# A two-layer decoder step on one core: heads' gate rows through DRAM, normalisers on GpSimd, the norm factors' row in two parts

## The chip, the cores and the metric

The kernel runs on one core of a Trainium2 chip. The metric is the device time of one execution in microseconds. Before the change the median of three runs is 953.47 us (953.25 to 953.63).

## The reference

The reference is one inference step of a two-layer decoder of width 1024, for a prompt of 256 tokens and for 8 samples of 8 new tokens each, with shared weights. Layer 0 mixes tokens by a gMLP (spatial gating in chunks of 128), layer 1 by an mLSTM matrix memory with eight heads. Each is followed by a gated MLP with a causal convolution, each part begins with an RMSNorm, and a last norm stands at the end. The memory layer, where most of the change lies, computes for each head and chunk:

```python
b = jnp.cumsum(fc, axis=-1)
D = b[..., :, None] - b[..., None, :] + ic[..., None, :]
inter = b + m[..., None]
m_t = jnp.maximum(inter, jnp.max(D, axis=-1))
w_intra = jnp.exp(D - m_t[..., None])
w_inter = jnp.exp(inter - m_t)
sc = jnp.einsum('bhtd,bhsd->bhts', qc, kc) * w_intra
num = w_inter[..., None] * jnp.einsum('bhtd,bhde->bhte', qc, C) + jnp.einsum('bhts,bhse->bhte', sc, vc)
den = w_inter * jnp.einsum('bhtd,bhd->bht', qc, n) + jnp.sum(sc, axis=-1)
h = num / jnp.maximum(jnp.abs(den), jnp.exp(-m_t))[..., None]
...
g = jnp.exp(bL[..., None] - b + ic - m_new[..., None])
kg = kc * g[..., None]
C_new = decay[..., None, None] * C + jnp.einsum('bhsd,bhse->bhde', kg, vc)
n_new = decay[..., None] * n + jnp.sum(kg, axis=2)
```

C is the state of 128 x 256 of a head and n its normaliser; both are outputs, for the prompt and for each sample.

## The kernel before

All 320 tokens are columns, and the features lie on the partitions. Weights stream from DRAM in blocks of 128 x 1024 (512 KB), issued by SyncE in the order of use. `take()` loads four blocks ahead and splits one ahead into a high and a low part of the fp32r format: ScalarE casts (`wh`, L167) and VectorE subtracts (`wl`, L168). `rows` (L189) makes three fp32r matmuls of each piece of 128 rows, and a `block` of eight such pieces is 24 matmuls of 320 columns into one bank of the pool `psm` (three banks, rows named `pm`). All other products go to the five banks of `psa`. The order of TensorE's instructions is that of the program. On the other engines the tile scheduler sets the order; `behind(...)` holds an instruction behind named ones.

**Norms.** Each norm sums squares over the features with TensorE (`norm_cols`, L242, tile `pc`) and takes the power −1/2 on GpSimd (`rc`, L254). `norm_row` (L270) turns the three columns of factors into a row on all partitions: VectorE puts them on diagonals (`dg`, L276 and L277), TensorE multiplies with ones (`pb`) and ScalarE copies the result (`rb`). It is called four times, once in each layer.

**Memory layer** (`layer_b`, L690). `gates` computes a matrix of 8 heads x 392 gate values (`Xf`: the running maximum of 320 tokens, 64 factors of the samples, 8 decays) and a second one, `RS`, that TensorE turns into columns (`pt`, `cols`). Then each head h runs through these steps, in a loop that works on the end of head h − 1 beside the start of head h:

- `qk_epi`, `v_epi`, `o_epi` end the weight blocks: convolution, activation, splits (`qh`, `kh`, `vTb`, `th_o`).
- `scores` spreads the head's row of `X` to all partitions with a matmul on a selector (`pMb`), forms the products `psc`, the weights `w` (exponentials on ScalarE, mask on GpSimd at L876), and their product `Pf` with its split `Ph`, `Pl` and sample parts `Pr`, `Ps`.
- `k_nat` and `v_nat` turn keys and values (`pk`, `pv`, written at L51) and scale them: `kz` (L916 and L917), `kgh` and `kgl` (L921, L922), `vh` and `vl` (L901, L902).
- `inter` and `state_sample` read the samples' states (`num`, `pcs`); `state_out` decays them (ScalarE, L957) and adds `pcs` (VectorE, L958). `numer` and `state_prompt` (`pCp`) follow; two small matmuls with `mkr` give the samples' normaliser sums, copied to `nPS`.
- `stats` takes mean, variance and scale (`sl` on GpSimd, L988), `nb` and the normed rows `hn`; `finish` turns these (`phn`), gates them (`y_b`) and splits them (`yhb` L1028, `ylb` L1029).

Heads 4 to 6 carry early blocks of the output product; after head 7 the rest follows.

Of the kernel before, what the change touches and what calls it, by code (L numbers as in the profile page):

```python
# [16 lines left out]
P = 128  # L17
# [21 lines left out]
class Net:  # L39
# [230 lines left out]
    def norm_row(self):  # L270

        nc = self.nc
        dg = self.tp.tile([P, T], F32, tag="sq", name="dg", bufs=2)
        pb = self.psa.tile([P, 512], F32, tag="pa", name="pb")
        for t in range(2):
            nc.vector.tensor_scalar(dg[:, t * P:(t + 1) * P], self.ident, self.rc[:, t:t + 1], None, op0=MULT)  # L276
        nc.vector.tensor_scalar(dg[:, TP:], self.ident[:, 64:], self.rc[:, 2:3], None, op0=MULT)  # L277
# [43 lines left out]
    def layer_a(self):  # L321
        nc, tc, I, O = self.nc, self.tc, self.I, self.O
        with tc.tile_pool(name="ya", bufs=1) as yp, tc.tile_pool(name="la", bufs=1) as lp:
# [80 lines left out]
            for q in range(4):  # L404
                pv = [self.psa.tile([P, 512], F32, tag="pa", name="pv") for _ in range(2)] + \
                    [self.psm.tile([P, 512], F32, tag="pm", name="pvs")]
                k = 0
                while k < KD:
                    (wh, wl), kn = self.take()
                    wh, wl = [x.rearrange("p (k e) c -> p k (e c)", e=4) for x in (wh, wl)]  # L410
                    for i in range(kn):
                        if q == 0 and k + i + 1 < KD:
                            self.enter(k + i + 1)
                        columns(q, k + i, pv, wh[:, i, :], wl[:, i, :])
                    k += kn
# [12 lines left out]
                if q > 0:  # L428
                    v_gelu(q, pv)
                waiting = pv  # L430
# [259 lines left out]
    def layer_b(self):  # L690
# [5 lines left out]
        with ExitStack() as ctx:  # L696
# [7 lines left out]
            X = lp.tile([P, 392], F32R, name="X")  # L704
            sel = lp.tile([P, NH, P], F32R, name="sel")
# [5 lines left out]
            nPS = lp.tile([P, NH, 10], F32, name="nPS")  # L711
            mkr = lp.tile([P, NB], F32R, name="mkr")
# [12 lines left out]
            def gates(rp):  # L725
# [3 lines left out]
                selr = rp.tile([40, NH, P], F32, name="selr")  # L729
# [5 lines left out]
                nc.sync.dma_start(selr, I["sel"])  # L735
# [4 lines left out]
                nc.gpsimd.memset(X.bitcast(F32), 0.0)  # L740
                nc.gpsimd.memset(sel.bitcast(F32), 0.0)
# [8 lines left out]
                Xf = row("Xf", 392)  # L750
# [46 lines left out]
                nc.scalar.activation(RS[32:40, 0:T], g, AF.Exp)  # L797
                nc.scalar.activation(RS[64:72, 0:T], m, AF.Exp, scale=-1.0)
# [5 lines left out]
                ps = self.block(KD, self.x_rhs)  # L804
                pt = self.psa.tile([P, 512], F32, tag="pa", name="pt")
# [48 lines left out]
            def scores(h):  # L854
# [3 lines left out]
                pb = self.psa.tile([P, 512], F32, tag="pa", name="pMb")  # L858
                mm(pb[:, :392], sel[:, h, :], X, True, True)
# [4 lines left out]
                dec = decs[:, h, :]  # L864
                nc.scalar.copy(dec, pb[:, 384:392])
# [6 lines left out]
                for (o, c0, t) in ((0, 0, 0), (TP, P, 1)):  # L872
                    nc.scalar.activation(w[:, o:o + TP - c0], pb[:, c0:TP], AF.Exp, scale=-1.0, bias=colsT[:, t, h:h + 1])
                nc.scalar.activation(w[:, 384:], w[:, 384:], AF.Exp, scale=-1.0)
                for o in (0, TP):
                    nc.gpsimd.affine_select(w[:, o:o + P], w[:, o:o + P], pattern=[[1, P]], compare_op=ALU.is_ge, fill=0.0,  # L876
                                            base=0, channel_multiplier=-1)
                Pf = hp.tile([P, 448], F32, tag="Pf", name="Pf", bufs=1)
# [3 lines left out]
                nc.vector.scalar_tensor_tensor(Pf, sc[:, :448], 0.25 * KSC, w, op0=MULT, op1=MULT)  # L882
                self.split(Ph, Pl, Pf[:, :384])

# [4 lines left out]
                s["P"] = (Ph, Pl, dec)  # L889
# [14 lines left out]
            def k_nat(h, bank=None):  # L904
                s = S[h]
                ks = s["k"][0]
                pk = bank or self.psa.tile([P, 512], F32, tag="pa", name="pk")
                for t in range(3):
                    self.tr(pk[:, t * P:(t + 1) * P], ks[:, t * P:(t + 1) * P] if t < 2 else s["ks"], self.ident)
                kgh = hp.tile([P, 2, P], F32R, tag="kgh", name="kgh", bufs=1)  # L910
                kgl = hp.tile([P, 2, P], F32R, tag="kgl", name="kgl", bufs=1)
                kz = hp.tile([P, 2, P], F32R, tag="kz", name="kz", bufs=1)
                src = pk[:, 2 * P:3 * P]

                for i in range(2):
                    nc.scalar.activation(kz[:, i, :], src, AF.Copy, scale=gm[:, i, h:h + 1])  # L916
                    nc.vector.scalar_tensor_tensor(kz[:, i, :], src, gm[:, 2 + i, h:h + 1], kz[:, i, :].bitcast(F32), op0=MULT, op1=ADD)  # L917
                for t in range(2):
                    g = colsT[:, t, 32 + h:33 + h]
                    src = pk[:, t * P:(t + 1) * P]  # L920
                    nc.scalar.activation(kgh[:, t, :], src, AF.Copy, scale=g)  # L921
                    nc.vector.scalar_tensor_tensor(kgl[:, t, :], src, g, kgh[:, t, :].bitcast(F32), op0=MULT, op1=SUB)  # L922
                s["kg"] = (kgh, kgl, kz)

# [50 lines left out]
            def stats(h):  # L975
# [12 lines left out]
                nc.gpsimd.tensor_tensor(sl, rd, self.mhalf.to_broadcast([P, 3]), op=ALU.pow)  # L988
                nb = hp.tile([P, 3], F32, tag="nb", name="nb", bufs=1)
# [5 lines left out]
            def state_prompt(h):  # L995
# [19 lines left out]
            def finish(h):  # L1015
# [3 lines left out]
                for e in range(2):  # L1019
# [9 lines left out]
                    nc.vector.scalar_tensor_tensor(yl[:, e, :], y, g, yh[:, e, :].bitcast(F32), op0=MULT, op1=SUB)  # L1029
# [51 lines left out]
            k_nat(0)  # L1081
            v_nat(0)
            for h in range(1, NH):
# [10 lines left out]
                if h == 1:  # L1094
                    hand_over(0)
                qk_epi(h, 1, ps)
# [3 lines left out]
                if h == 1:  # L1100
                    close(0)
                else:
                    with self.behind_split():
                        stats(h - 1)
                v_epi(h, 0, ps)
                early(h, 2)
                if h == 1:
                    stats(0)
                else:
                    with self.behind(S[h]["halves"][1]):  # L1110
                        self.prefetch(0, self.used + 2)
                with self.behind(*S[h]["halves"]):
                    ps = blk()
                v_epi(h, 1, ps)
# [13 lines left out]
                v_nat(h)  # L1128
                if h == 1:
                    finish(0)  # L1130
                if not last:
                    with self.behind(S[h]["vh"], S[h]["vl"]):
                        ps = blk()
                    o_epi(h, 1, ps)
                    hand_over(h)
# [15 lines left out]
            nc.gpsimd.tensor_tensor(nS, nS, nPS[:, :, 2:], op=ADD)  # L1151
            nc.sync.dma_start(O["nP"], nPS[:, :, 0])
# [64 lines left out]
def _lay_out(i):  # L1217
# [64 lines left out]
    sel = np.zeros((40, NH, P), f)  # L1282
    for h in range(NH):
        sel[h, h] = 1.0
        sel[32 + h, h] = 1.0
    a["sel"] = sel
# [33 lines left out]
```

## Time and profile before

| | |
|---|---|
| median of three runs | 953.47 us |
| the profiled execution | 953.45 us |
| its span, first to last instruction | 951.7 us |
| TensorE clock granted | 0.998 |
| busy: TensorE, VectorE, ScalarE, GpSimd | 945.0, 670.9, 519.1, 83.9 us |
| one head of the memory layer (the third) | 27.85 us |

In the profile PE is TensorE's matmul, PEld its weight load, DVE VectorE, ACT ScalarE, POOL GpSimd and SP SyncE. A row of the timeline gives start and length in us, engine, line, operation, output and inputs by the program's names, partitions x elements, and a count of equal neighbours; in square brackets stand the idle time ahead of it and what ended it. Matmuls overlap, so their cost is read from start to start.

### The profile page before, as it was taken

The numbers are of one execution on the slowest core, as the hardware profiler recorded it, in microseconds if no ns is written. First come the engines' busy times: TensorE is split into PE (matmuls) and PEld (weight loads), VectorE is DVE, ScalarE is ACT, GpSimd is POOL, SyncE is SP. The second block draws the span as 40 slices with busy tenths as digits, with TensorE's granted clock in tenths as the row PEclk, the third lists the DMA queues.
The fourth block names the chain that finished last, engine by engine and source line by source line (L and its number), as shares of the span: only waits on it lengthen the run. The fifth ranks groups of instructions, "written<-read, shape, count | busy, mean of one in ns | idle before, by whom it ended". The sixth has DMA issues, their size and how long they took to land.

```text
span 951.7 us, 17271 instructions
## 1 busy us (share of the span) xinstructions
PE 945.0 (99%) x6571; PEld 923.4 (97%) x6571; DVE 670.9 (70%) x1237; ACT 519.1 (55%) x952; POOL 83.9 (9%) x277
## 2 busy tenths in 40 slices
PE   9999999999999999999999999999999999999997
PEld 8789999999999999999999999999999999999997
DVE  6568985577777764458898987776777777775542
ACT  6467444354455543347787776575755555444332
POOL 2200000010000000012211001000101111100001
PEclk9999999999999999999999999999999999999999
DMA  8646344444444445456557556634474444445621
GB/s 286 212 133 186 122 140 150 144 150 150 143 151 156 151 147 148 145 179 215 183 209 224 167 193 205 202 116 163 112 246 156 153 155 146 144 148 152 200 83 56
DMA packets 58073, 155.25 MB, mean 163 GB/s; under 512 B 7670, under 2 KB 19574, under 8 KB 57990
## 3 DMA queue, kind: packets, MB, share of 16 engines
q1 hardware_dynamic: 57846, 153.89, 50.6%
q8 instruction: 52, 0.85, 0.4%
q14 instruction: 31, 0.25, 0.1%
q10 hardware_dynamic: 144, 0.26, 0.1%
HBM read 142.19 MB, written 11.94 MB: 162 GB/s over the span
## 4 chain that ended last, share of the span: by engine, by line
PE 99%; POOLq 0%; ACT 0%; DVE 0%; DVEq 0%; issue 0%; ACTq 0%
PE pm L48 83%; PE pv L48 5%; PE num L48 2%; PE pvs L48 2%; PE pyt L48 1%; PE pmix L48 1%; PE py L48 1%; PE pCp L48 1%; PE psc L48 1%; PE pcs L48 1%; PE pv L51 1%; PE phn L51 0%; PE pw L48 0%; PE pk L51 0%; PE pc L48 0%; PE pg L48 0%
## 5 line engine op out<-in xcount | busy, mean ns | idle before, releaser
L167 ACT CAST wh<-raw 128x1024 fp32r<-128x1024 f32 (+4 forms) x252 | 254.3, 1013 | 286.7 <-PE pm L48 170.2
L48 PE MATMUL pm<-xh,wh 128*128 128x320 f32 x1216 | 379.5, 312 | 0.0
L168 DVE TENSOR_TENSOR wl<-raw,wh 128x1024 fp32r<-128x1024 f32 (+4 forms) x252 | 295.9, 1179 | 118.5 <-ACT wh L167 116.0
L48 PE MATMUL pm<-xh,wl 128*128 128x320 f32 x1216 | 375.8, 309 | 0.0
L48 PE MATMUL pm<-xl,wh 128*128 128x320 f32 x1216 | 375.6, 309 | 0.0
L48 PEld LDWEIGHTS pm<-xh,wh 128*128 128x128 f32 x1216 | 228.4, 188 | 0.7
L48 PEld LDWEIGHTS pm<-xl,wh 128*128 128x128 f32 x1216 | 228.4, 188 | 0.2
L48 PEld LDWEIGHTS pm<-xh,wl 128*128 128x128 f32 x1216 | 228.3, 188 | 0.0
L48 PE MATMUL pm<-yh_f,wh 128*128 128x320 f32 x308 | 95.3, 309 | 0.0
L48 PE MATMUL pm<-yl_f,wh 128*128 128x320 f32 x308 | 94.9, 308 | 0.0
L48 PE MATMUL pm<-yh_f,wl 128*128 128x320 f32 x308 | 94.9, 308 | 0.0
L48 PEld LDWEIGHTS pm<-yl_f,wh 128*128 128x128 f32 x308 | 57.8, 188 | 0.0
L48 PEld LDWEIGHTS pm<-yh_f,wh 128*128 128x128 f32 x308 | 57.8, 188 | 0.0
L48 PEld LDWEIGHTS pm<-yh_f,wl 128*128 128x128 f32 x308 | 57.8, 188 | 0.0
L536 DVE SCALAR_TENSOR_TENSOR fcv<-fpad,vecs,fcv 128x336 f32<-128x336 f32 x88 | 49.6, 565 | 2.2 <-ACT fcv L534 0.7
L301 DVE TENSOR_TENSOR xT<-pm,xT 128x320 f32<-128x320 f32 x38 | 18.6, 490 | 31.7 <-PE pm L48 31.7
L48 PE MATMUL pm<-yhb,wh 128*128 128x320 f32 x128 | 40.2, 314 | 0.0
L48 PE MATMUL pm<-yh_a,wh 128*128 128x320 f32 x128 | 39.6, 309 | 0.0
L48 PE MATMUL pm<-yh_a,wl 128*128 128x320 f32 x128 | 39.5, 309 | 0.0
L48 PE MATMUL pm<-yl_a,wh 128*128 128x320 f32 x128 | 39.5, 308 | 0.0
L48 PE MATMUL pm<-ylb,wh 128*128 128x320 f32 x128 | 39.5, 308 | 0.0
L48 PE MATMUL pm<-yhb,wl 128*128 128x320 f32 x128 | 39.4, 308 | 0.0
(317 smaller groups left out, 1356.8 us busy)
## 6 DMA issues: line engine op xcount, KB each, us to landing
raw<-in_f_up SPq DMA_DIRECT2D x88, 512.0 KB, 3.5
raw<-in_b_win SPq DMA_DIRECT2D x48, 512.0 KB, 4.7
raw<-in_f_dn SPq DMA_DIRECT2D x28, 448.0 KB, 3.2
C<-in_C SPq DMA_DIRECT2D x32, 258.0 KB, 5.4
raw<-in_a_win SPq DMA_DIRECT2D x16, 512.0 KB, 3.8
raw<-in_a_wo SPq DMA_DIRECT2D x16, 512.0 KB, 3.6
out_Cs<-C SPq DMA_DIRECT2D x32, 256.0 KB, 5.7
raw<-in_f_dn SPq DMA_DIRECT2D x14, 512.0 KB, 3.5
```

Source lines behind the costliest of these rows:

```text
L48: self.pin(self.nc.tensor.matmul(out, lhsT, rhs, start=start, stop=stop))
L51: self.pin(self.nc.tensor.transpose(out, in_, ident))
L167: self.last_split = nc.scalar.copy(wh[:, c, :], raw[:, c, :])
L168: self.last_low = nc.vector.tensor_tensor(wl[:, c, :], raw[:, c, :], wh[:, c, :].bitcast(F32), op=SUB)
L301: self.nc.vector.tensor_tensor(x, ps[:, :T], x, op=ADD)
L536: nc.vector.scalar_tensor_tensor(cv, pd[:, i:i + NC], self.vec(w + i * KF), cv, op0=MULT, op1=ADD)
```

## The change

1. **`norm_row`**: the factors are split in a high and a low fp32r part, with a diagonal for each, and two fp32r matmuls replace the one in full precision. In layer A the call moves behind the next group of columns.
2. **`gates`**: the first three matmuls of the first q block stand ahead of the column sums. `X`, `sel` and `mkr` go, with their loads, fills and casts. Head 0's row is spread by a full-precision matmul of `Xf`, on 128 partitions with zeros, with a selector `first`, ahead of the turns `pt`.
3. **Rows through DRAM**: `Xf` and a part of `RS` are written to a tensor `rows` of 8 x 456 in DRAM; `rows_in(h)` reads one head's row back onto all partitions (tile `mb`, two buffers), a head ahead. `scores(h)` reads it in place of `pMb` for h > 0.
4. **Normalisers**: the matmuls with `mkr` go. GpSimd multiplies the samples' keys with the row's factors (`nk`, 128 x 64), copies the decays (`decs`) and the prompt's normaliser (`nP`). At the end VectorE sums `nk` and adds.
5. **Order**: the later half of `scores` becomes `weigh`; `pk` takes a bank of `psm` in all heads; `v_nat(h)` follows `finish(h − 1)` from head 2 on; in the last head `finish(6)` stands ahead of `weigh(7)`; in head 1 `stats(0)` is cut in two and `hand_over` moves.

```diff
     def norm_row(self):
-        dg = self.tp.tile([P, T], F32, tag="sq", name="dg", bufs=2)
+        rc = self.tp.tile([P, 2, 3], F32R, tag="rc2h", name="rc_hl", bufs=1)
+        self.split(rc[:, 0, :], rc[:, 1, :], self.rc)
+        dg = self.tp.tile([P, 2, T], F32R, tag="dg", name="dg", bufs=1)
+        rc = rc.bitcast(F32)
+        for half in range(2):
+            nc.vector.tensor_tensor(
+                dg[:, half, :TP].rearrange("p (t c) -> p t c", c=P), self.ident.unsqueeze(1).to_broadcast([P, 2, P]),
+                rc[:, half, :2].unsqueeze(2).to_broadcast([P, 2, P]), op=MULT)
+            nc.vector.tensor_scalar(dg[:, half, TP:], self.ident[:, 64:], rc[:, half, 2:3], None, op0=MULT)
...
-        self.mm(pb[:, :T], self.ones, dg, True, True)
+        for half in range(2):
+            self.mm(pb[:, :T], self.ones.bitcast(F32R), dg[:, half, :], half == 0, half == 1)
...
                 if q == 1:
-                    self.norm_row()
                     load_ws()
                 if q == 2:
+                    self.norm_row()
                     row_sums()
...
+                p0 = self.psm.tile([P, 512], F32, tag="pm", name="pm")
+                (wh, wl), _ = self.take()
+                self.rows(p0, wh, wl, 1, self.x_rhs, True, False)
                 self.norm_cols()
-                p0 = self.block(KD, self.x_rhs)
+                self.rows(p0, wh[:, 1:, :], wl[:, 1:, :], 7, lambda k: self.x_rhs(1 + k), False, True)
                 self.norm_row()
...
-                nc.vector.tensor_copy(X[0:8], Xf)
-                nc.vector.tensor_tensor(X[32:40], Xf, X[0:8].bitcast(F32), op=SUB)
-                nc.scalar.copy(sel[:40], selr)
-                nc.vector.tensor_copy(mkr, mk[:, :NB])
+                nc.sync.dma_start(I["rows"][:, :392], Xf)
...
+                nc.sync.dma_start(I["rows"][:, 392:], RS[32:40, TP:T])
+                rows_in(0)
+                rows_in(1)
...
                 ps = self.block(KD, self.x_rhs)
+                pb = self.psa.tile([P, 512], F32, tag="pa", name="pMb")
+                mm(pb[:, :392], first, Xz, True, True)
+                S[0]["spread"] = pb
                 pt = self.psa.tile([P, 512], F32, tag="pa", name="pt")
...
-                pb = self.psa.tile([P, 512], F32, tag="pa", name="pMb")
-                mm(pb[:, :392], sel[:, h, :], X, True, True)
+                rows = s["rows"]
+                pb = s.get("spread", rows)
...
+                if h:
+                    with self.behind(s["masked"]):
+                        sums(h)
...
+            def sums(h):
+                s = S[h]
+                if h:
+                    nc.gpsimd.tensor_copy(decs[:, h, :], s["rows"][:, 384:392])
+                nc.gpsimd.tensor_tensor(nk[:, h, :], s["k"][0][:, TP:T], s["rows"][:, 392:], op=MULT)
+
+            def weigh(h):
+                Ph, Pl, _ = S[h]["P"]
+                Pf, Pr = S[h]["Pf"]
                 self.split(Ph, Pl, Pf[:, :384])
...
+            def rows_in(h):
+                S[h]["rows"] = lp.tile([P, 456], F32, tag="mb", name="mb", bufs=2)
+                nc.sync.dma_start(S[h]["rows"], I["rows"][h:h + 1, :].to_broadcast([P, 456]))
...
-                for i in range(2):
-                    mm(pc[:, CW:CW + NB], kz[:, i, :], mkr, i == 0, i == 1)
-                Cp = hp.tile([P, DV], F32, tag="Cp", name="Cp", bufs=1)
-                nc.scalar.copy(Cp, pc[:, :DV])
-                nc.sync.dma_start(O["Cp"][h], Cp)
-                nc.scalar.copy(nPS[:, h, :], pc[:, DV:DV + 10])
+                Cp = hp.tile([P, CW], F32, tag="Cp", name="Cp", bufs=1)
+                nc.scalar.copy(Cp, pc[:, :CW])
+                nc.sync.dma_start(O["Cp"][h], Cp[:, :DV])
+                nc.gpsimd.tensor_copy(nP[:, h:h + 1], Cp[:, DV:DV + 1])
...
             scores(0)
-            k_nat(0)
+            k_nat(0, self.psm.tile([P, 512], F32, tag="pm", name="pk"))
             v_nat(0)
+            with self.behind(S[0]["vl"]):
+                weigh(0)
...
+                if not last:
+                    rows_in(h + 1)
                 v_epi(h, 0, ps)
...
                 scores(h)
-                k_nat(h, self.psm.tile([P, 512], F32, tag="pm", name="pk") if h == 1 else None)
+                if last:
+                    finish(h - 1)
+                weigh(h)
+                k_nat(h, self.psm.tile([P, 512], F32, tag="pm", name="pk"))
+                if 1 < h and not last:
+                    finish(h - 1)
                 if h > 1:
-                    finish(h - 1)
+                    v_nat(h)
...
-            nc.gpsimd.tensor_tensor(nS, nS, nPS[:, :, 2:], op=ADD)
-            nc.sync.dma_start(O["nP"], nPS[:, :, 0])
+            ns = lp.tile([P, NH, NB], F32, name="ns")
+            with self.behind(S[h]["yl"]):
+                nc.vector.tensor_reduce(ns, nk.rearrange("p h (b s) -> p h b s", s=NS), axis=mybir.AxisListType.X, op=ADD)
+            nc.vector.scalar_tensor_tensor(nS, ns, 0.5 * KSC, nS, op0=MULT, op1=ADD)
+            nc.sync.dma_start(O["nP"], nP)
```

How this moves instructions is seen at three places. The first is TensorE in the gates, from the last matmuls of the gate block (`pg`) over the column sums (`pc`) into the first q block (`pm`). Before:

```order
L48 MATMUL pg<-xh,wl 128x320
L48 MATMUL pg<-xl,wl 128x320
L48 MATMUL pc<-ones,acc 128x2 x3
L48 MATMUL pm<-xh,wh 128x320
L48 MATMUL pm<-xl,wh 128x320
L48 MATMUL pm<-xh,wl 128x320
```

After, at the same place:

```order
L48 MATMUL pg<-xh,wl 128x320
L48 MATMUL pg<-xl,wl 128x320
L48 MATMUL pm<-xh,wh 128x320
L48 MATMUL pm<-xl,wh 128x320
L48 MATMUL pm<-xh,wl 128x320
L48 MATMUL pc<-ones,acc 128x2 x3
```

The three matmuls of the first piece of the q block have moved ahead of the column sums.

The second place is VectorE in head 0, from the second product with the convolution's taps to the last low part of the keys (`kgl`). Before:

```order
L831 SCALAR_TENSOR_TENSOR bcv<-bpad_4513,vecs,bcv 128x344
L882 SCALAR_TENSOR_TENSOR Pf<-psc,w 128x448
L917 SCALAR_TENSOR_TENSOR kz<-pk,gm,kz 128x128
L902 SCALAR_TENSOR_TENSOR vl<-pv,rc_4619,vh 128x256
L310 TENSOR_TENSOR Pl<-Pf,Ph 128x384
L886 SCALAR_TENSOR_TENSOR Ps<-Pf,mk,Pr 128x4x16
L922 SCALAR_TENSOR_TENSOR kgl<-pk,cols,kgh 128x128
L902 SCALAR_TENSOR_TENSOR vl<-pv,rc,vh 128x256
L922 SCALAR_TENSOR_TENSOR kgl<-pk,cols,kgh 128x128
```

After (line numbers are those of the changed file), from the weight split and the copy of `cols` on; between the two pieces the dots leave out `Qz`, `w`, `gm` and two `vl`:

```order
L168 TENSOR_TENSOR wl<-raw,wh 128x1024
L819 COPY cols<-pt 128x288
...
L899 SCALAR_TENSOR_TENSOR Pf<-psc,w 128x448
L944 SCALAR_TENSOR_TENSOR kz<-pk,gm,kz 128x128
L929 SCALAR_TENSOR_TENSOR vl<-pv,rc,vh 128x256
L316 TENSOR_TENSOR Pl<-Pf,Ph 128x384
L944 SCALAR_TENSOR_TENSOR kz<-pk,gm,kz 128x128
L914 SCALAR_TENSOR_TENSOR Ps<-Pf,mk,Pr 128x4x16
L842 SCALAR_TENSOR_TENSOR bcv<-bpad_4521,vecs,bcv 128x344
L834 TENSOR_TENSOR bpad_4517<-pm,rb 128x256
L949 SCALAR_TENSOR_TENSOR kgl<-pk,cols,kgh 128x128
```

The last `vl` and both `kz` now stand ahead of the first `kgl`; in before one `vl` stood between the two `kgl`, and one split fewer stood ahead of the copy of `cols`.

The third place is ScalarE in head 2, around the casts of values (`vh`) and keys (`kgh`). Before:

```order
L921 ACTIVATE kgh<-pk,cols 128x128 x2
L901 ACTIVATE vh<-pv,rc 128x256
L901 ACTIVATE vh<-pv,rc_4619 128x256
L1012 ACTIVATE th_o<-o_b 128x320
L901 ACTIVATE vh<-pv,rc 128x256
L167 CAST wh<-raw 128x1024 x3
```

After:

```order
L928 ACTIVATE vh<-pv,rc_4632 128x256
L928 ACTIVATE vh<-pv,rc 128x256
L948 ACTIVATE kgh<-pk,cols 128x128
L887 ACTIVATE w<-mb,cols 128x256
L1064 ACTIVATE yhb<-y_b,gnh 128x320
L948 ACTIVATE kgh<-pk,cols 128x128
L887 ACTIVATE w<-mb,cols 128x128
L928 ACTIVATE vh<-pv,rc 128x256
L167 CAST wh<-raw 128x1024
```

The exponentials of head 3 (`w`, from the row `mb` that DRAM gave) stand here between the casts of head 2; in before a head's exponentials stood ahead of its own `kgh`.

More of the change, by code (lines that the diff above doesn't have):

```diff
@@ L710, in layer_b @@
             decs = lp.tile([P, NH, NB], F32, name="decs")
-            nPS = lp.tile([P, NH, 10], F32, name="nPS")
-            mkr = lp.tile([P, NB], F32R, name="mkr")
+            nP = lp.tile([P, NH], F32, name="nP")
+            nk = lp.tile([P, NH, 64], F32, name="nk")
             pads = []
@@ L728, in gates @@
                 rst = rp.tile([40, 2, T], F32, name="rst")
-                selr = rp.tile([40, NH, P], F32, name="selr")
+                Xz = rp.tile([P, 392], F32, name="Xf")
+                first = rp.tile([P, P], F32, name="first")
                 RS = rp.tile([P, T], F32, name="RS")
@@ L749, in gates @@
                 ig, z, az = zi[:8], zi[32:], az[32:]
-                Xf = row("Xf", 392)
+                Xf = Xz[:8]
+                nc.gpsimd.memset(Xz, 0.0)
+                nc.gpsimd.memset(first, 0.0)
+                nc.gpsimd.memset(first[0:1, :], 1.0)
                 a, M = RS[0:8, 0:T], Xf[:, 0:T]
@@ L863, in scores @@
                 mm(sc[:, 384:448], s["ks"], q[:, TP:T], True, True)
-                dec = decs[:, h, :]
-                nc.scalar.copy(dec, pb[:, 384:392])
+                dec = rows[:, 384:392]
+                if h == 0:
+                    dec = decs[:, 0, :]
+                    nc.scalar.copy(dec, pb[:, 384:392])
                 Qd = Qz.rearrange("p (g i r) -> p g i r", g=4, i=2)[:, :, :, :NS]
@@ L988, in stats, with scaled @@
                 nc.gpsimd.tensor_tensor(sl, rd, self.mhalf.to_broadcast([P, 3]), op=ALU.pow)
+                s["sl"] = num, mv, sl
+                if h:
+                    scaled(h)
+            def scaled(h):
+                s = S[h]
+                num, mv, sl = s.pop("sl")
                 nb = hp.tile([P, 3], F32, tag="nb", name="nb", bufs=1)
@@ L1095, in layer_b @@
                     hand_over(0)
+                    with self.behind(S[0]["masked"]):
+                        sums(0)
                 qk_epi(h, 1, ps)
@@ L1108, in layer_b @@
                     stats(0)
-                else:
-                    with self.behind(S[h]["halves"][1]):
-                        self.prefetch(0, self.used + 2)
+                with self.behind(S[h]["halves"][1]):
+                    self.prefetch(0, self.used + 2)
                 with self.behind(*S[h]["halves"]):
                     ps = blk()
+                if h == 1:
+                    with self.behind_split():
+                        scaled(0)
                 v_epi(h, 1, ps)
                 scores(h)
-                k_nat(h, self.psm.tile([P, 512], F32, tag="pm", name="pk") if h == 1 else None)
+                if last:
[4 more added lines that the diff above has]
+                    finish(h - 1)
                 if h > 1:
-                    finish(h - 1)
+                    v_nat(h)
                 early(h, 3)
@@ L1281, in _lay_out @@
     a["seg"] = seg
[L1282 to L1286, printed above, removed]
     tok = s // 32 * 16 + s % 16
@@ L1304 @@
     O = {k: nc.dram_tensor("out_" + k, s, F32, kind="ExternalOutput").ap() for k, s in _OUTS.items()}
+    I["rows"] = nc.dram_tensor("rows", (8, 456), F32, kind="Internal").ap()
     with tile.TileContext(nc) as tc:
```

29 lines of the change are left out of this document (13 added, 16 removed).

## Prediction

> **What bounds the kernel now.** I read the page first: the busy time of each engine and the chain that ended last.
>
> ```profile
> span 951.7 us, 17271 instructions
> PE 945.0 (99%) x6571; PEld 923.4 (97%) x6571; DVE 670.9 (70%) x1237; ACT 519.1 (55%) x952; POOL 83.9 (9%) x277
> ...
> PE 99%; POOLq 0%; ACT 0%; DVE 0%; DVEq 0%; issue 0%; ACTq 0%
> ...
> L168 DVE TENSOR_TENSOR wl<-raw,wh 128x1024 fp32r<-128x1024 f32 (+4 forms) x252 | 295.9, 1179 | 118.5 <-ACT wh L167 116.0
> ```
>
> TensorE works 945.0 of 951.7 us and carries 99% of the chain. A mean over stages can hide one with another limit, so I then asked for the waits of TensorE and for the windows of one head of the memory layer.
>
> ```profile
> PE pw L48 <- PEq L1302: 0.8, 1, 0.8
> ```
>
> ```profile
> 486.80:514.65 27.85, 27.85 (x221) 26.93 (x220) 25.53 (x58) 21.94 (x52) 4.38 (x11) 1.00 0.65 212
> ```
>
> The columns of the second are the stretch, its length, then busy time of PE, PEld, DVE, ACT, POOL, then granted clock, DMA share and GB/s. In this head TensorE is busy for all 27.85 us, VectorE for 25.53 and ScalarE for 21.94. So the memory layer is TensorE's too, but VectorE has only 2.3 us to spare in a head. The list of waits shows one, at the start; but ends of matmuls are modelled, so a short wait hides in a "busy" row. I therefore take prices and hidden waits from **start to start** of neighbouring rows. The rule for the sum: a matmul removed is time removed, unless a new wait takes it; work on the other engines is free as long as what it makes is ready when TensorE gets there.
>
> **Change, part by part.**
>
> *The factors' row.* TensorE's rows around one of the four calls:
>
> ```profile
> 197.26 0.31 PE L48 MATMUL pm<-xh,wl 128*128 128x320 f32 x1
> 197.41 0.70 PE L48 MATMUL pb<-dg,ones 128*128 128x320 f32 x2
> 197.71 0.56 PE L48 MATMUL pm<-xh,wh 128*128 128x320 f32 x1
> 198.10 0.30 PE L48 MATMUL pm<-xl,wh 128*128 128x320 f32 x1
> ```
>
> One fp32r matmul of 320 columns steps 197.41 − 197.26 = 0.15 us. The full-precision product is recorded as two matmuls; from its start to the second block matmul behind it is 198.10 − 197.41 = 0.69, less one ordinary step, 0.54. Two fp32r matmuls are 2 × 0.15 = 0.29 (0.147 unrounded). Each call saves 0.25, four save **−1.0**. The price is the diagonal, made twice and after a cast and a subtraction. The tightest call is that of the gates:
>
> ```profile
> 427.78 0.85 POOL L254 TENSOR_TENSOR rc<-ms,mhalf 128x3 f32<-128x3 f32 x1 [0.17 <-DVE ms L253]
> ...
> 428.66 0.48 DVE L276 TENSOR_SCALAR dg<-ident,rc 128x128 f32<-128x128 f32 x2 [0.88 <-POOL rc L254]
> 429.06 0.25 DVE L277 TENSOR_SCALAR dg<-ident,rc 128x64 f32<-128x64 f32 x1
> ```
>
> ```profile
> 430.26 0.70 PE L48 MATMUL pb<-dg,ones 128*128 128x320 f32 x2
> ```
>
> The diagonal is ready at 429.31 and used at 430.26: 0.95 us of cover. A half costs VectorE the same 0.65 (428.66 to 429.31); a cast and a subtraction of three columns in a row, some 0.3 to 0.4. In the gates the whole starts about 0.2 later (below) and TensorE arrives about 0.25 earlier, so the first half comes about on time and the second (needed 0.15 later) 0.1 to 0.2 late. The bounds are no wait and, if each call lost the whole 0.25 again, +1.0. I take +0.1 here and +0.1 in layer A, where a weight split now stands behind the moved call, +0.2 together.
>
> *The normaliser's matmuls.* Each of eight heads loses two:
>
> ```profile
> 486.66 0.28 PE L48 MATMUL pCp<-mkr,kz 128*128 128x8 f32 x2
> 486.80 0.40 PE L48 MATMUL pm<-xh,wh 128*128 128x320 f32 x1
> 487.03 0.31 PE L48 MATMUL pm<-xl,wh 128*128 128x320 f32 x1
> ```
>
> From their start to the second matmul behind them is 0.37, less one step of 0.15: 0.22 a head, **−1.8** for eight. Their work goes to GpSimd, whose cost is a rival below.
>
> *The heads' rows.* Heads 1 to 7 lose the matmul that spreads a head's row:
>
> ```profile
> 497.45 0.34 PE L48 MATMUL pMb<-X,sel 128*128 128x392 f32 x1
> 497.63 0.28 PE L48 MATMUL psc<-qh,kh 128*128 128x256 f32 x1
> ```
>
> 0.18 each, seven of them: **−1.26**. The scores then start 0.18 earlier and need their k split so much sooner. Head 0 spreads its row in full precision. No such matmul of 392 columns is in the trace: below it lies the 0.18 above (no loss), above it four times that, 0.72; the nearest row is the full-precision pb, 0.54 × 392/320 = 0.67 by width. I take 0.67, so **+0.49**.
>
> *The gates' first matmuls* now stand ahead of the column sums:
>
> ```profile
> 425.56 0.41 PE L48 MATMUL pg<-xl,wl 128*128 128x320 f32 x1
> 425.97 0.83 PE L48 MATMUL pc<-ones,acc 128*128 128x2 f32 x6
> ```
>
> The sums start 0.41 after the last matmul of the gates instead of 0.15: TensorE waits 0.26 for the squares. Three block matmuls (0.44) fill it and put the sums 0.18 later: **−0.26**, between that and nothing.
>
> *Head 0's states* wait in before; head 1 shows the same work without most of the wait:
>
> ```profile
> 458.00 1.08 PE L48 MATMUL num<-C,Qz 128*32 128x258 f32 x16
> 459.00 0.90 PE L48 MATMUL pcs<-vh,kz 32*128 32x256 f32 x4
> ...
> 460.19 0.41 PE L48 MATMUL pm<-xh,wh 128*128 128x320 f32 x1
> ```
>
> ```profile
> 479.31 1.08 PE L48 MATMUL num<-C,Qz 128*32 128x258 f32 x16
> ...
> 481.00 0.42 PE L48 MATMUL pm<-xh,wh 128*128 128x320 f32 x1
> ```
>
> 2.19 against 1.69, so 0.50 of wait. What comes late is on VectorE:
>
> ```profile
> 458.60 0.48 DVE L902 SCALAR_TENSOR_TENSOR vl<-pv,rc,vh 128x256 fp32r<-128x256 f32 x1
> 459.12 0.35 DVE L922 SCALAR_TENSOR_TENSOR kgl<-pk,cols,kgh 128x128 fp32r<-128x128 f32 x1
> ```
>
> The last kgl ends at 459.47 and frees the bank of pk, which pcs takes. After the change pk lies in another pool, and on VectorE the last vl and kz stand ahead of both kgl. Against it, one more weight split (1.18, L168 of the page) stands ahead of the copy of cols. Adding up the rows in the new order brings the last kz to about 458.4; TensorE wants it at about 459.0. I take the gain, **−0.50**; the bounds are that, and a further 0.6 lost if the split is not absorbed.
>
> *The last head.* TensorE's rows around the late half of an output operand:
>
> ```profile
> 671.43 0.31 PE L48 MATMUL pm<-yhb,wh 128*128 128x320 f32 x1
> 671.65 0.41 PE L48 MATMUL pm<-ylb,wh 128*128 128x320 f32 x1
> 671.90 0.31 PE L48 MATMUL pm<-yhb,wl 128*128 128x320 f32 x1
> ```
>
> Steps of 0.22 and 0.25 in place of 0.15 each. The finishing work of head 6 now stands ahead of the last head's products on VectorE: **−0.17**, or nothing.
>
> *The values' turns* stand together with those of the normed rows. They are no cheaper for it:
>
> ```profile
> 502.89 0.82 PE L51 MATMUL pv<-ident,vTb 128*128 128x128 f32 x6
> 503.47 0.39 PE L48 MATMUL pm<-xh,wh 128*128 128x320 f32 x1
> ```
>
> Six take 0.58, 0.097 each, and any grouping keeps all six: 0.
>
> **Sum.** −1.0 − 1.76 − 1.26 + 0.49 − 0.26 − 0.50 − 0.17 + 0.2 = −4.26. The profiled execution took 953.45 us (span 951.7 and 1.75 around it), 0.02 under the median of 953.47. So 949.2.
>
> **Rivals.**
>
> *Rows late (slower).* The exponentials of the next head's weights now read the row that comes from DRAM, and on ScalarE, which keeps order, they stand between the casts kgh and the last vh of the present head. A row that is late holds vh, then vl, and with them pcs on TensorE, in heads 1 to 6. To come out slower than before, 4.26 plus the 1.9 of the bound must be lost in six heads, over 1.0 us a head. In time of before, SyncE issues the row just behind the states' outputs, and ScalarE wants it before:
>
> ```profile
> 485.63 0.97 SPq L959 DMA_DIRECT2D out_Cs<-C  x2
> ```
>
> ```profile
> 504.90 0.48 ACT L901 ACTIVATE vh<-pv,rc 128x256 fp32r<-128x256 f32 x1
> ```
>
> ```profile
> bst<-in_b_state SPq DMA_DIRECT2D x1, 192.0 KB, 2.5
> out_Cs<-C SPq DMA_DIRECT2D x32, 256.0 KB, 5.7
> ```
>
> That is about 18 us for a landing of 2.5 to 5.7: 12 us of cover. It would have to land in over 19 us, or be held that long in SyncE's queue. At a head's loss of 1.2 the time is 949.2 + 7.2 = 956.4. Chance 0.06.
>
> *GpSimd and VectorE in each other's way.* The new product nk is 128x64, and the nearest rows are
>
> ```profile
> L1150 POOL TENSOR_TENSOR nS<-n,decs 128x64 f32<-128x64 f32 x1 | 0.9, 854 | 6.6 <-ACT decs L865 6.6
> ```
>
> ```profile
> L826 POOL COPY bns<-bpad x16: 187/314/1247, 433.5 to 658.5; 128x3 f32<-128x3 f32 x16
> ```
>
> Alone it is 0.85 us. The second row (shortest, median, longest) shows one tiny copy between 0.19 and 1.25, so a neighbour can add 1.06. In head 1 nk stands on GpSimd ahead of sl, from which the normed rows come; in later heads behind it. If each of eight heads lost as much as a neighbour can add, less the 0.95 of cover of the kind seen above, plus up to 1.0 once in head 1, it would be 8 × 0.11 + 1.0 = 1.9, so 951.1. [...] Chance 0.10.
>
> *The waits stay (little gain).* If head 0, the gates and the last head keep their waits (0.93), the factors' rows give back 1.0, the split costs head 0 its 0.6 more, and the states of head 0 come 0.5 late to the prompt's matmuls, the change is −4.46 + 3.0 = −1.4, or 952.0: within 0.2%, about what a measurement of this kernel can tell from no change. Chance 0.10.
>
> *Head 1 slower by its new order*, the only head whose finishing is rearranged by hand: a wait of 1 us there gives 950.2, inside the forecast.
>
> **Numbers.** Forecast 949.2 with chance 0.74; its own bounds are a little more hidden waiting removed (947.8) and one or two of the waits kept (950.6). The rivals have 0.06, 0.10 and 0.10. The range for 8 in 10 reaches from 947.8 to 951.8: it takes in the second rival and leaves out most of the first and third. 0.2% is 1.9 us, so faster means under 951.56: the forecast, the second rival for the most part and a little of the third, 0.85. Same: most of the third, 0.08. Slower: 0.07.
>
> **What would show it.** In the profile after: pb in two fp32r matmuls 0.3 from start to start; no matmul on mkr; one pMb, 0.67 long, ahead of the turns pt; pg to pc at 0.15; head 0 from num to the next block like head 1's 1.69; heads of 27.45 in place of 27.85; TensorE still busy all through. I am wrong if a head keeps its 27.85, if ScalarE is shown waiting for mb, if a start-to-start gap opens at pcs, phn or psc in every head, or if pb waits for dg.

## The result, and the profile after

The changed kernel takes 949.30 us (median of six runs, 949.04 to 949.94) against 953.21 for the kernel before (six runs, 952.82 to 953.63). The ratio is 0.996 with a 95% interval of 0.9947 to 0.9972: 3.9 us faster, where 949.2 was forecast. The page of the changed kernel still says that TensorE is all there is:

```profile
span 947.7 us, 17236 instructions
...
PE 940.8 (99%) x6549; PEld 919.5 (97%) x6549; DVE 675.1 (71%) x1244; ACT 517.7 (55%) x940; POOL 85.1 (9%) x300
...
PE 99%; ACT 0%; POOLq 0%; DVE 0%; issue 0%; DVEq 0%; ACTq 0%
```

TensorE's busy time fell by 4.2 us and the span by 4.0. One head (from the second matmul of a block to the same one in the next head) went from 27.85 to 27.42 us, with TensorE busy all through:

```profile
485.47:512.89 27.42, 27.42 (x218) 26.50 (x217) 25.21 (x58) 21.16 (x49) 5.17 (x14) 1.00 0.71 232
```

The total says little about single steps. Since TensorE keeps the order of the program, one can put the start of the same matmul in both traces side by side; the difference changes only where a step was added, removed or made to wait.

| TensorE starts | before | after | difference | since the row above | forecast |
|---|---|---|---|---|---|
| layer A, pv, ahead of any change | 33.73 | 33.42 | −0.31 | −0.31 | none |
| layer A, pv, behind its factors' row | 64.56 | 64.33 | −0.23 | +0.08 | −0.25 + 0.1 |
| gates, pg (behind the first ConvFFN) | 423.23 | 422.77 | −0.46 | −0.23 | −0.25 |
| gates, q block behind pc | 427.33 | 426.62 | −0.71 | −0.25 | −0.26 |
| gates, second pc (behind pb) | 430.80 | 429.91 | −0.89 | −0.18 | −0.25 + 0.1 |
| head 0, num (behind spread, scores) | 458.00 | 457.58 | −0.42 | +0.47 | +0.49 |
| head 0, second num (behind pcs) | 463.81 | 462.89 | −0.92 | −0.50 | −0.50 |
| last head, late output operand | 669.38 | 665.49 | −3.89 | −2.97 | −2.80 |
| last head, num | 672.14 | 668.08 | −4.06 | −0.17 | −0.17 |
| second ConvFFN, pc | 711.64 | 707.49 | −4.15 | −0.09 | −0.22 |
| second ConvFFN, behind pb | 716.51 | 712.58 | −3.93 | +0.22 | −0.25 |
| turns of the output, pyt | 941.78 | 937.72 | −4.06 | −0.13 | none |

The first row is no effect of the change: it arises at 4 to 7 us, where the first product starts at 4.09 before and 3.99 after, and pairs of matmuls step 0.43 us, up to 6.81 before and 6.27 after, in place of 0.24 later; and at 10 us the traces of the experiments below lie between 0.3 us ahead of the changed kernel's and 0.9 us behind it. So spans of single executions are compared from 10 us on. The row "second ConvFFN, behind pb" has the wrong sign. In the kernel before, TensorE took 0.68 us from pb to the second block matmul behind it:

```profile
715.83 0.70 PE L48 MATMUL pb<-dg,ones 128*128 128x320 f32 x2
716.12 0.55 PE L48 MATMUL pm<-xh,wh 128*128 128x320 f32 x1
716.51 0.31 PE L48 MATMUL pm<-xl,wh 128*128 128x320 f32 x1
```

In the changed kernel it takes 0.81 (712.58 − 711.77), as its rows from the block matmul ahead of pb on show:

```profile
711.53 0.31 PE L48 MATMUL pm<-xh,wl 128*128 128x320 f32 x1
711.77 0.82 PE L48 MATMUL pb<-dg,ones 128*128 128x320 f32 x2
712.43 0.31 PE L48 MATMUL pm<-xh,wh 128*128 128x320 f32 x1
```

The two cheap matmuls of pb take 0.66 us from start to start, where 0.29 was worked out, and begin 0.09 late. What they wait for is two steps back, on GpSimd and VectorE:

```profile
708.38 1.52 POOL L532 COPY fpad<-fst 128x16 f32<-128x16 f32 x3 [3.37 <-DMA fst<-in_f_state]
709.86 0.85 POOL L254 TENSOR_TENSOR rc<-ms,mhalf 128x3 f32<-128x3 f32 x1
```

```profile
708.62 1.23 DVE L168 TENSOR_TENSOR wl<-raw,wh 128x1024 fp32r<-128x1024 f32 x1 [0.21 <-ACT wh L167]
...
711.88 0.25 DVE L281 TENSOR_SCALAR dg<-ident,rc_hl 128x64 fp32r<-128x64 f32 x1
```

Three small copies take 1.52 us beside a weight split that ends at 709.85, and the power for the factors stands behind them; so the last diagonal ends at 712.13, when the second matmul should have started at 711.8. In the kernel before, the split stands behind the diagonals on VectorE, not ahead of them. It starts 1.4 us after the copies have ended, so they (first line, GpSimd) met no split (second line, VectorE):

```profile
712.46 0.47 POOL L526 COPY fpad<-fst 128x16 f32<-128x16 f32 x3 [3.30 <-DMA fst<-in_f_state]
```

```profile
714.34 1.22 DVE L168 TENSOR_TENSOR wl<-raw,wh 128x1024 fp32r<-128x1024 f32 x1
```

So the changed order on VectorE exposed the copies to the split. In layer A the step to a matmul with low parts is 0.44 and the next one 0.33, in place of 0.23 each:

```profile
55.07 0.40 PE L48 MATMUL pv<-wh,xl 128*128 128x512 f32 x1
55.51 0.50 PE L48 MATMUL pv<-wl,xh 128*128 128x512 f32 x1
55.84 0.40 PE L48 MATMUL pv<-wh,xh 128*128 128x512 f32 x1
```

### The profile page after: what moved, and what is told of

The parts are those of the page before. It is cut to its first block, busy times and chain, and to the rows that moved or that the text cites. A ratio compares the mean times of both kernels' runs of the same rounds, so it can differ in the third digit from the quotient of the medians.

```text
span 947.7 us, 17236 instructions
## 1 busy us (share of the span) xinstructions
PE 940.8 (99%) x6549; PEld 919.5 (97%) x6549; DVE 675.1 (71%) x1244; ACT 517.7 (55%) x940; POOL 85.1 (9%) x300
## 4 chain that ended last, share of the span: by engine, by line
PE 99%; ACT 0%; POOLq 0%; DVE 0%; issue 0%; DVEq 0%; ACTq 0%
PE pm L48 83%; PE pv L48 5%; PE num L48 2%; PE pvs L48 2%; PE pyt L48 1%; PE pmix L48 1%; PE py L48 1%; PE psc L48 1%; PE pCp L48 1%; PE pcs L48 1%; PE pv L51 1%; PE phn L51 0%; PE pw L48 0%; PE pk L51 0%; PE pg L48 0%; PE pc L48 0%
```

## The experiments

All start from the changed kernel; e_fix and e_best ran five times, the others once. "From 10 us on" is the difference in the start of the same matmul against its trace.

**e_ffn: who stands ahead of the power.**

```diff
-                nc.gpsimd.tensor_copy(ps_[:, :, 0:2], stt[:, b, :].rearrange("p (b e) -> p b e", e=2))
+                with self.behind(*([self.rc_done] if b < 3 else [])):
+                    nc.gpsimd.tensor_copy(ps_[:, :, 0:2], stt[:, b, :].rearrange("p (b e) -> p b e", e=2))
```

> The changed kernel, with GpSimd's first three copies of convolution state in each ConvFFN ordered behind the power for the norm factors. In the second ConvFFN of the changed kernel the factors' row costs 0.22 us instead of saving 0.25. Theory A: one of these copies is held for 1.04 us beside a weight split on VectorE, and the power waits behind it on GpSimd. Then here the power ends near 709.3 instead of 710.7, the diagonals are ready before TensorE arrives, and from the norm on all is 0.45 us earlier (span 947.2). Theory B: the longer chain on VectorE (cast, subtraction, four products, behind a weight split) is by itself too long for the cover; then the step of pb stays near 0.7 and nothing is gained (span 947.7).

The power now runs first, and the matmuls are 0.29 from start to start:

```profile
708.19 0.85 POOL L254 TENSOR_TENSOR rc<-ms,mhalf 128x3 f32<-128x3 f32 x1 [3.48 <-DVE ms L253]
709.00 1.18 POOL L533 COPY fpad<-fst 128x16 f32<-128x16 f32 x3
```

```profile
711.38 0.46 PE L48 MATMUL pb<-dg,ones 128*128 128x320 f32 x2
711.67 0.31 PE L48 MATMUL pm<-xh,wh 128*128 128x320 f32 x1
```

From there on everything is 0.46 earlier; the span is 946.9. Theory A: the longer chain of diagonals fits once the power is in time. The copies are again long (1.18) beside the split, and now nobody waits.

**e_pre: a weight split of layer A asked for one step earlier.**

```diff
                     row_sums()
+                    self.prefetch(0, self.used + 2)
```

> The changed kernel, with one weight split of layer A asked for one step earlier, ahead of the third column group's activations. Theory A: the wait of 0.33 us in layer A (a low-part matmul at 55.5) comes from ScalarE, where the copy of the factors' row and an activation stand ahead of the weight cast; then the wait goes and all behind it is 0.3 us earlier (span 947.4). Theory B: VectorE's statistics and sums set the split's time; then nothing changes (span 947.7), or the earlier cast holds up the banks of the column group and TensorE loses up to 0.5.

The step in layer A is 0.23 and 0.22, and all behind it is 0.32 earlier: theory A.

```profile
54.75 0.39 PE L48 MATMUL pv<-wh,xl 128*128 128x512 f32 x1
54.98 0.39 PE L48 MATMUL pv<-wl,xh 128*128 128x512 f32 x1
55.20 0.39 PE L48 MATMUL pv<-wh,xh 128*128 128x512 f32 x1
```

This kernel also gains 0.46 at the second ConvFFN, where nothing was touched. Its GpSimd and VectorE rows there say why:

```profile
707.18 0.48 POOL L533 COPY fpad<-fst 128x16 f32<-128x16 f32 x3 [2.82 <-DMA fst<-in_f_state]
707.84 0.85 POOL L254 TENSOR_TENSOR rc<-ms,mhalf 128x3 f32<-128x3 f32 x1 [0.18 <-DVE ms L253]
```

```profile
707.97 1.23 DVE L168 TENSOR_TENSOR wl<-raw,wh 128x1024 fp32r<-128x1024 f32 x1 [0.21 <-ACT wh L167]
```

The same three copies take 0.48 us, because their data landed early enough for them to run ahead of the split. Of the seven traces with this code unrepaired, those of the changed kernel, e_bank and e_mm lost there, and those of e_pre, e_late, e_nk and e_idle gained 0.46 against the changed kernel: with the split at this place, it depends on when a transfer lands.

**e_full: the factors' row as before**, in one full-precision matmul and at its old place (`norm_row` is that of the kernel before).

> The changed kernel with the factors' row as before: one full-precision matmul, one diagonal, at its old place in layer A; all else as changed. By the prediction's price (0.25 a call, 0.2 of waits) this is 0.8 us slower than the changed kernel (span 948.5). By the difference of the two traces (0.06 lost in layer A, 0.21 gained in the first ConvFFN, 0.18 in the gates, 0.22 lost in the second ConvFFN) it is 0.1 us slower (span 947.8).

955.14 us: a miss of both. In layer A and the ConvFFNs TensorE's starts agree with the kernel before, so the differences of the table stand. But the scheduler, with other instructions to place, put a weight split of the gates late:

```profile
PE pm L48 <- DVE wl L168: 2.6, 1, 2.6
PE pm L48 <- ACT wh L167: 0.9, 1, 0.9
```

TensorE waits 3.4 us there, and loses 1.6 us more behind it, in which the granted clock (third column from the end) is down:

```profile
445.00:449.00 4.00, 4.00 (x17) 4.00 (x18) 2.41 (x3) 1.68 (x2) 0.10 (x1) 0.57 0.41 129
```

So the run's total does not price the factors' row; the table does. One more thing is seen in it: between the rows "second ConvFFN, behind pb" and "turns of the output" of the table it loses 0.14 against the changed kernel, as the kernel before does (0.13), and no other experiment loses anything there.

**e_bank: head 0's keys back in a bank that pcs takes.**

```diff
-            k_nat(0, self.psm.tile([P, 512], F32, tag="pm", name="pk"))
+            k_nat(0)
```

> The changed kernel with head 0's turned keys pk back in a bank of the five that pcs takes. Theory A (the prediction's): pcs waits for the last low part of the keys, because it frees that bank; VectorE ends it near 460.3 to 460.9 in the new order, while pcs starts at 458.6, so TensorE loses 1.5 to 2.2 us there (span about 949.5). Theory B: what counts is only that the values' low parts come earlier on VectorE; then nothing is lost (span 947.7).

954.06 us, a span of 952.2. The wait is that of theory A, but the span is 2.7 us above the one expected, in good part because again the clock falls behind the wait:

```profile
PE pcs L48 <- DVE kgl L949: 1.7, 1, 1.7
```

```profile
461.30:465.30 4.00, 3.95 (x25) 3.73 (x26) 3.58 (x10) 3.83 (x11) 0.55 (x2) 0.57 0.04 13
```

From 10 us on, 2.4 us are lost up to the first pcs matmuls that follow (0.4 of it already where the values are turned) and another 1.5 in matmuls behind it, the block matmuls among them with steps of 0.27 instead of 0.147. So in the new order the bank counts; whether it would have been enough by itself, in the old order, no run shows.

**e_idle: what a wait costs.** Four waits of growing length in the first ConvFFN:

```diff
+            def stall(n, ps):
+                with tc.issue_after(self.last_split.ins):
+                    nc.scalar.copy(slow[0], ps[:, :T])
+                    for i in range(n):
+                        nc.scalar.copy(slow[(i + 1) % 2], slow[i % 2])
+                pz = self.psa.tile([P, 512], F32, tag="pa", name="pz")
+                self.mm(pz[:, :8], self.ident, slow[n % 2][:, :8], True, True)
```

> The changed kernel with four waits put into the first ConvFFN: at the end of a block TensorE makes one small matmul (its sum is not used) on a tile that ScalarE has copied 1, 3, 5 and 7 times in a row, 0.42 us each, so TensorE stands still for about 0.7, 1.5, 2.4 and 3.2 us. It asks what a wait costs: two kernels showed TensorE at a granted clock of 0.57 for 4 us after waits of 2.1 and 2.6 us. Theory A (a wait costs its length): block matmuls step 0.147 us right after each wait, loss 8 us in all. Theory B (a wait over some length between 0.5 and 2.1 us drops the clock): after the longer ones the steps are 0.27 us for some 16 matmuls, 1.5 to 2 us more each; the place where it begins tells the length.

The timeline gives the waits in brackets; the windows just behind each give the clock:

```profile
234.37 0.36 PE L48 MATMUL pz<-slow,ident 128*128 128x8 f32 x2 [1.40 <-issue]
...
265.33 0.39 PE L48 MATMUL pz<-slow,ident 128*128 128x8 f32 x2 [2.34 <-ACT slow L534]
...
297.30 0.39 PE L48 MATMUL pz<-slow,ident 128*128 128x8 f32 x2 [3.32 <-ACT slow L534]
...
332.00 0.60 PE L48 MATMUL pz<-slow,ident 128*128 128x8 f32 x2 [4.53 <-ACT slow L534]
```

```profile
234.60:237.60 3.00, 3.00 (x22) 3.00 (x22) 1.99 (x4) 0.46 (x1) 0.00 (x0) 1.00 0.47 123
265.60:268.60 3.00, 3.00 (x23) 3.00 (x23) 1.01 (x3) 0.46 (x1) 0.00 (x0) 1.00 0.60 175
297.60:302.20 4.60, 4.60 (x22) 4.60 (x22) 0.49 (x1) 0.04 (x1) 0.00 (x0) 0.63 0.27 105
332.50:336.50 4.00, 4.00 (x17) 4.00 (x17) 0.00 (x0) 0.00 (x0) 0.00 (x0) 0.53 0.04 14
```

Theory B, but here the granted clock was 1.00 behind the waits of 1.4 and 2.3 us and 0.63 and 0.53 behind those of 3.3 and 4.5, where the theory had it fall from somewhere between 0.5 and 2.1 on. Waits of 1.4 and 2.3 us cost their length (1.9 and 2.8 us with the small matmul). After 3.3 us (from 1.3 us behind the wait on) and after 4.5 us (at once) the matmuls step 0.27 for 12 and 13 of them, 1.5 and 1.8 us more. The waits came out longer than I had worked out from the copies alone.

**e_late, e_nk: the two rivals.**

```diff
-                if not last:
-                    rows_in(h + 1)
...
+                if h > 1:
+                    rows_in(h)
                 scores(h)
```

> The changed kernel with the read of a head's row from DRAM moved most of a head later, to just ahead of the scores of the same head (heads 2 to 7). In the changed kernel a row lands 4.9 us after its issue (483.6) and is first read at 500.5, so 12 us lie idle. Theory A (cover): issued some 10 to 14 us later it lands about when it is wanted, the exponentials move behind the casts that they would hold, and TensorE loses under 0.2 us a head, span below 949. Theory B (the rival): ScalarE waits for the row in its order, vh and vl come late and TensorE waits at pcs in six heads, 1 us or more each, span 953 or above.

```diff
+                for _ in range(5):
+                    nc.gpsimd.tensor_tensor(nk[:, h, :], s["k"][0][:, TP:T], s["rows"][:, 392:], op=MULT)
```

> The changed kernel with the GpSimd product nk made five times over in each head instead of once (the extra four repeat it, the result is the same). One took 0.32 us, so 1.3 us more a head on GpSimd, 10 us in all. Theory A (room): GpSimd is busy 85 of 948 us and nothing that TensorE waits for stands close behind; span 947.2 to 948.0. [...]

In e_late (949.66 us, span 947.9) every head starts where it does in the changed kernel, within 0.02 us once the 0.7 us of the first 10 us are taken off: theory A, as far as the run goes. The edit moved the reads by less than meant: those of heads 2 and 3 are issued where they were, those of heads 4 to 7 come 5.0 to 6.7 us later instead of 10 to 14. So about half of the idle 12 us was used up and TensorE lost nothing; a later row was not tried. In e_nk (span 947.5) head 2 loses 0.10 and no other head does, although the longest of the 40 products took 1.39 us, where the median took 0.33 (shortest, median, longest):

```profile
L908 POOL TENSOR_TENSOR nk<-qs,mb x40: 319/326/1390, 456.1 to 662.8; 128x64 f32<-128x64 f32 x40
```

**e_mm: the normaliser matmuls' price.**

```diff
+                for i in range(2):
+                    mm(pc[:, CW:CW + NB], kz[:, i, :], vh[:, i, :NB], i == 0, i == 1)
```

> The changed kernel with two matmuls of 8 columns put back behind each head's prompt state, as before the change but on other operands (their sums are not used). It prices the removed normaliser matmuls alone. By the prediction's rows 0.22 us a head: each head from 27.43 to 27.65, span 949.4. If the heads became shorter for another reason (their new order), the span stays at 947.7 to 948.2.

```profile
485.60 0.28 PE L48 MATMUL pCp<-vh,kz 128*128 128x8 f32 x2
485.74 0.40 PE L48 MATMUL pm<-xh,wh 128*128 128x320 f32 x1
485.98 0.31 PE L48 MATMUL pm<-xl,wh 128*128 128x320 f32 x1
```

Heads 0 to 6 each lose 0.24, the last one 0.07; from 10 us on 1.77 in all. So of the 0.43 that a head became shorter, the removed matmuls are 0.24; the spread of its row was 0.18 by its rows, which leaves next to nothing for the new order.

**e_fix and e_best: repairs.** e_fix joins the edits of e_ffn and e_pre. e_best also spreads head 0's row in one fp32r matmul, with low parts on partitions 32 to 39 and ones in row 0 and row 32 of the selector:

```diff
+                nc.vector.tensor_copy(Xz[0:8], Xf)
+                nc.vector.tensor_tensor(Xz[32:40], Xf, Xz[0:8].bitcast(F32), op=SUB)
```

> Both repairs in one: the copies of convolution state behind the power for the factors on GpSimd, and the weight split of layer A asked for one step earlier. If the two waits are independent, 0.33 less in layer A and up to 0.47 less at the second ConvFFN's norm, where the changed kernel loses it in those executions in which the copies land beside a weight split: 948.4 to 948.9 against 949.3 for the changed kernel, ratio to before 0.9950 to 0.9955. If one of them only moves the wait, 949.0 or more.

> Both repairs, and head 0's row spread in one fp32r matmul again: high parts of the rows on partitions 0 to 7, low parts on 32 to 39, and a selector that adds the two (two more VectorE instructions in the gates, as before the change). The spread cost 0.66 us in full precision and 0.18 before. If the two instructions fit beside the gates' work, head 0's scores start 0.48 us earlier than in the changed kernel, and with the repairs the time is 948.2 to 948.6, ratio to before 0.9945 to 0.9950. If they push the copy of the gate columns on VectorE, the later pcs of head 0 takes back up to 0.5 and the time is 948.7 to 949.1.

e_fix: 949.11 us (five runs, 948.79 to 949.62), ratio to before 0.9955 (0.9941 to 0.9968). The median lies outside the expected 948.4 to 948.9. Its trace is 0.79 us shorter from 10 us on, both waits gone, but its first 10 us were 0.9 longer; by times alone it cannot be told from the changed kernel. e_best: 948.53 us (947.99 to 948.66), ratio 0.9949 (0.9935 to 0.9962). The spread steps 0.18 instead of 0.66, and the gain of 0.47 against e_fix, counted from 10 us on, holds to the end:

```profile
450.70 0.34 PE L48 MATMUL pMb<-Xz,first 128*128 128x392 f32 x1
450.88 0.49 PE L51 MATMUL pt<-ident,RS 128*128 128x128 f32 x3
```

## Why the prediction was right, and where it was off

- **TensorE bounds all, a removed matmul is removed time:** held. The normaliser's matmuls and the rows' spread in seven heads gave 2.97 + 0.09 where 2.80 + 0.22 was forecast; each pair was worth 0.24 in place of 0.22 (e_mm), and in the last head only 0.09 of it came out, as e_mm lost only 0.07 there.
- **Head 0's row in full precision:** +0.47 against +0.49. Its matmul was 0.66 by its own rows:

```profile
451.25 0.82 PE L48 MATMUL pMb<-Xf,first 128*128 128x392 f32 x2
451.91 0.49 PE L51 MATMUL pt<-ident,RS 128*128 128x128 f32 x3
```

- **The gates' first matmuls, head 0's states, the last head's operand:** −0.25, −0.50, −0.17, each as forecast. Head 0's states now take 1.69 us to the next block, as head 1's did before:

```profile
457.58 1.08 PE L48 MATMUL num<-C,Qz 128*32 128x258 f32 x16
...
459.27 0.41 PE L48 MATMUL pm<-xh,wh 128*128 128x320 f32 x1
```

  e_bank showed that the bank is needed for this. The other two stand in the traces alone; no experiment tried them.
- **The factors' row** is the step that failed in size. Forecast were −1.0 and +0.2 of waits, −0.8; the table gives +0.08, −0.23, −0.18 and +0.22, so −0.11. The matmuls are as cheap as said (0.29 a call). The waits were 0.9 instead of 0.2: in layer A the weight cast that a copy and an activation delay (e_pre), and in the second ConvFFN a wait for which I had allowed nothing, in executions where GpSimd's copies meet a split (e_ffn). I had read the cover there from the diagonals alone, and neither from what stood ahead of the power on GpSimd nor from where the scheduler would put the split. In the four traces where the copies ran early the second ConvFFN gains 0.46 more, which would make −0.57 of the −0.11.
- **That the total came out at 0.1 us** from the forecast is partly luck. The change was forecast at 4.26 us and measured at 3.91; the time fits better than that because 949.2 was counted from 953.47, and the six runs of the kernel before have a median of 953.21. Between the two traces the miss of 0.7 is made up in good part by 0.31 at the start and 0.13 at the end, which no step of the forecast holds. The first is the chance of one execution. The second comes with the factors' row, since e_full, with the old row, is the only experiment without it; why is open.
- **The rivals.** Rows late: the cover of 12 us was real. In the changed kernel a row lands 4.9 us (median) after its issue, and that of head 3 is issued 17 us before ScalarE reads it (e_late took up about half of this cover):

```profile
mb<-rows SPq DMA_DIRECT2D x8, 228.0 KB, 4.9
```

```profile
483.58 0.34 SPq L954 DMA_DIRECT2D mb<-rows  x1
```

```profile
500.54 0.52 ACT L887 ACTIVATE w<-mb,cols 128x256 f32<-128x256 f32 x1
```

  GpSimd and VectorE: work of GpSimd did take longer beside a split (the three copies 1.52 us, in place of 0.48 in e_pre), but in the changed kernel that was not nk. One nk took 0.32 us (at most 0.34), not 0.85; the row that I took for its price had a split beside it, and the same product takes 0.32 in the changed kernel (first line: VectorE in the kernel before; second: the changed kernel):

```profile
666.06 1.23 DVE L168 TENSOR_TENSOR wl<-raw,wh 128x1024 fp32r<-128x1024 f32 x1 [0.79 <-ACT wh L167]
```

```profile
L1202 POOL TENSOR_TENSOR nS<-n,decs x1: 323/323/323, 629.5 to 629.5; 128x64 f32<-128x64 f32 x1
```

  Waits that stay: this rival was right about a good part of the factors' row only; the other three waits went. Head 1, rearranged by hand, shows no wait of its own: from 466.0 to 486.8 us of before it gains 0.42, like the heads behind it. The rivals were priced at the length of their waits. For waits of 1.0 to 1.2 us at pcs, as in the first, no run shows whether that is enough: 1.7 us there cost the clock as well (e_bank), 1.4 us between block matmuls did not (e_idle).

## What to carry to other kernels

Where one engine's order is fixed, list the start of the same instruction in both traces: each step of a sum is then checked by itself, and errors that cancel in the total come to light. When a step is moved, read what stands ahead of its first link on each engine, the small engine too, and whether the time of that work depends on when a transfer lands. A wait of TensorE can cost more than its length: here 1.4 and 2.3 us between block matmuls cost just that (e_idle), while 3.3 and 4.5 us (e_idle), 0.9 and 2.6 us in a row (e_full) and 1.7 us behind narrow matmuls (e_bank) cost another 1.5 to 1.8 us of lower clock.

## What the runs showed of the hardware

- **GpSimd copies took longer beside a VectorE split.** The copy of 128x16 took 0.20 us in the median of 44 and at most 1.24, among the three beside the split that starts at 708.62 (shortest, median and longest of the changed kernel):

```profile
L532 POOL COPY fpad<-fst x44: 198/200/1240, 139.8 to 839.3; 128x16 f32<-128x16 f32 x44
```

  These three end at 709.90, 0.05 us after the split. The power of three columns took no longer: in e_ffn and e_pre it took its 0.85 while a split began 0.13 us behind it, and that split took its usual 1.23.
- **TensorE's clock fell after some waits.** The granted clock was 0.63 in the 4.6 us and 0.53 in the 4 us just behind waits of 3.3 and 4.5 us (e_idle), 0.57 in 4 us behind waits of 0.9 and 2.6 in a row (e_full), and 0.57 in 4 us behind one of 1.7 that followed narrow matmuls of 32 rows or columns (e_bank). It was 1.00 in the 3 us behind waits of 1.4 and 2.3 (e_idle). So the clock fell behind 1.7 us in one place and not behind 2.3 in another; what makes the difference, and where the border lies, no run shows.
